# Small numbers in one shared tile, and the norms of queries and keys applied to the attention scores

## The chip, the cores and the metric

The kernel runs on one core of a Trainium2 chip. The metric is the time of one execution on the device in microseconds (us). The kernel before was timed in three runs: 2431.29, 2431.8 and 2432.54 us, median 2431.8 us.

## The reference

One layer of a streaming encoder on 256 tokens of width 2048, all in fp32. In order:

```
x += 1/2 * SwiGLU(norm(x))                  # d_ff = 5632, called ffn1 in the kernel
h  = norm(x); proj = h @ w_in               # six inputs of two recurrent branches, and gates
y_A = HGRN2 recurrence; y_B = conv(4) -> RG-LRU * gelu gate
x += (sigmoid(gate_A) * (y_A @ w_branch_a) + sigmoid(gate_B) * (y_B @ w_branch_b)) @ w_out
x += CrossAttention(norm(x), norm(mem))     # 4 heads of 512, 256 memory tokens
x += 1/2 * SwiGLU(norm(x))                  # called ffn2
return norm(x)
```

The part that the change rewrites is the cross-attention's scores:

```
q = norm(x) @ wq;  k, v = split(norm(mem) @ wkv)
s = einsum('bshd,bmhd->bhsm', q, k) * (512 ** -0.5)
p = softmax(s, axis=-1);  o = einsum('bhsm,bmhd->bshd', p, v);  x += o @ wo
```

A norm is `x * rsqrt(mean(x*x) + eps) * gain`. The gain works on a feature; the root works on a token, so it can be multiplied into any later result of a matrix product, row by row: for q, a row is a query token, for k a memory token.

## The kernel before

**Precision.** Every fp32 operand is split in two tiles, a rounded high part (`h`, `xh`, written by ACT) and the rest (`l`, `xl`, written by DVE as the difference), and a product of two numbers is three matmuls: high by high, high by low, low by high. A matmul here is 128 rows by 128 stationary columns by 512 (or 256) moving columns; its first operand in a row's name is what moves or what stays, the names are only sorted. Weights come in pieces of 1 MB (`raw`, 128x2048) over the queue of SP, are split by ACT and DVE, and are used by PE once. In the two feed-forward parts most pieces are multiplied by a scheme with seven instead of eight block products, for which DVE also makes differences (`td`, `made`) and splits them (`tl`).

**Order.** The program is first recorded as a list of operations. `Flow.arrange` then plays it through with a price for each operation and sets the order on every engine and the buffer that each tile takes; `Flow.emit` writes the instructions in that order. So one operation less or more can move others. All instructions carry line 478, where they are emitted; rows are told apart by the tiles' names.

**Places.** Tiles lie in pools, one behind the other in each partition, each tile starting on the next multiple of 32 bytes. In the built program before, the order is: constants (`vt`, `ones`, `eps`, the residual `x0` to `x3`, `rmtok`, `par`); nine tiles of 8192 bytes in the pool `big`; 24 tiles of 4096 bytes in `slots`; the small tiles (`sst`, `stdt`, `ssm`, `rtok`, `root`, `st`); then the scoped pools. In the feed-forward parts the scoped pool is `more`, four further tiles of 8192 bytes that are used as `big` ones are. In the middle it holds `tmp`, `scores`, `extra`, `feature`. Weights (`h`, `l`, `tl`) therefore lie in `big` or in `more`, as buffers come free; the other operand of a feed-forward matmul (`xh`, `xl`, `hidop`) lies in `slots`, and `ms`, the memory tokens, in `big` or `more`.

**The middle's norms.** `product` (the planner's queries, keys and input projection) gives 512 columns, 256 of high and 256 of low tokens; `summed` adds the two halves (ACT copies one to `lo`, DVE adds) and, with `by`, multiplies by a tile `rstd` of 128x256 that holds a token's root in each column. `by_feature` makes such a tile: two DVE operations write `diag`, an fp32 matmul with `ones` spreads it, ACT copies it out. `rtok` and `rmtok` hold the roots of the text and the memory tokens as columns, one number for each partition. `scores(h)` computes a head: for each of two groups of 128 queries, 4 x 2 matmuls, `summed` into `p`, the maximum of each row, its negative into `st`, ACT's exponential with that as bias, the reciprocal of the sum, and DVE's multiplication by it. Four transposes per head (`acc<-vt,p`) then turn `p` for the product with the values (`ps`, `vs`).

Of the kernel before, what the change touches and what calls it, by code (L numbers as in the profile page):

```python
# [9 lines left out]
F32 = mybir.dt.float32  # L10
F32R = mybir.dt.float32r
ACT = mybir.ActivationFunctionType
ALU = mybir.AluOpType

P = 128
T = 256
D = 2048
# [6 lines left out]
HD = D // HEADS  # L24
# [15 lines left out]
PAD = 16  # L40
# [149 lines left out]
class Flow:  # L190
# [22 lines left out]
    def pool(self, name, bufs, scope=None, **kw):  # L213
        self.pools.append(Pool(self, name, bufs, scope, **kw))
        return self.pools[-1]
# [267 lines left out]
def block_kernel(tc: tile.TileContext, xT, xin, memT, mem, vec, gfin, bgate, lruw, wu1, wd1, win, wv,  # L483
                 wg, wab, wout, wq, wk, wvm, wo, wu2, wd2, out_):
    flow = Flow(tc)
    pe, dve, act, sp, gps = flow.queues
    pool = flow.pool

    const = pool("const", 1)
    flow.share("big", pool("big", 9), 9)  # L490

    def big(name, dt=F32R):
        return flow.shared("big", [P, 2048], dt, name)

    slots = pool("slots", 24)
    small = pool("small", 2)
# [16 lines left out]
    def slot(dt=F32, name="slot"):  # L513
        return slots.tile([P, 1024], dt, name=name, tag="slot")

    def t1(name="t1"):
        return scoped["tmp"].tile([P, T], F32, name=name, tag="t1")

    def bank(name="acc"):
        return psum.tile([P, 512], F32, name=name, tag="acc")  # L520
# [6 lines left out]
    def col(name, i=0, n=1):  # L527
        a = VEC[name][0] + i
        return vt[:, a:a + n]
# [3 lines left out]
    warm = bank("warm")  # L533
    for _ in range(16):
        pe.matmul(warm[:, :P], ones, ones, start=True, stop=True)
    eps = const.tile([P, 1], F32, name="eps")
    act.activation(eps, ones[:, :1], ACT.Copy, scale=EPS)
    xt = [const.tile([P, 4 * T], F32, name=f"x{q}") for q in range(4)]
    x = [xt[k // 4][:, (k % 4) * T:(k % 4 + 1) * T] for k in range(KT)]
# [57 lines left out]
    def weights(*key):  # L597
        while plan and len(ahead) < 2:
            i = next(planned)
            k, src, kind = plan.pop(0)  # L600
            flow.room = room["scope"] if k[0] in orders else None
            if i in head:
                head[i]()
            if plan and plan[0][2] == "added":
                begun.append(begin_added(plan[0][1]))
            ahead.append((k, prepare(src, kind, 4 if i < 4 else 1)))
            if i in rest:
                rest[i]()
            make_ahead(i - between[0])
        k, w = ahead.pop(0)  # L610
        assert k == key, (k, key)
        return w
# [72 lines left out]
    def product(xs, w, late=()):  # L685

        acc = bank()
        h, l = w

        def high(ks):  # L690
            for k in ks:
                pe.matmul(acc, h[:, k * P:(k + 1) * P], xs[k], start=k == 0, stop=False)

        def low(ks):
            for k in ks:
                done["product"] = pe.matmul(acc[:, :T], l[:, k * P:(k + 1) * P], xs[k][:, :T], start=False,
                                            stop=k == KT - 1).ins

        high(range(KT - 4))
        was_late = bool(late)  # L700
        if was_late:
            flush(late)
            low(range(KT - 4))
        high(range(KT - 4, KT))
        low(range(KT - 4 if was_late else 0, KT))
        return acc
# [15 lines left out]
    def summed(acc, out=None, by=None):  # L722

        lo = t1("lo")
        act.activation(lo, acc[:, T:], ACT.Copy)
        out = t1("sum") if out is None else out
        dve.tensor_tensor(out=out, in0=acc[:, :T], in1=lo, op=ALU.add)
        if by is not None:
            dve.tensor_tensor(out=out, in0=out, in1=by, op=ALU.mult)
        return out  # L730
# [105 lines left out]
    def by_feature(r):  # L836

        diag = t1("diag")
        for t in range(2):
            dve.tensor_scalar(out=diag[:, t * P:(t + 1) * P], in0=ident, scalar1=r[:, t:t + 1], scalar2=None,  # L840
                              op0=ALU.mult)
        acc = bank()
        pe.matmul(acc[:, :T], ones, diag, start=True, stop=True)
        o = scoped["feature"].tile([P, T], F32, name="rstd", tag="rstd")
        act.activation(o, acc[:, :T], ACT.Copy)
        return o
# [233 lines left out]
            self.tiles.append(self.cur[:, i * 512:(i + 1) * 512])  # L1080
            return self.tiles[-1]

    ms1, rmtok = BigOperands(), const.tile([P, 2], F32, name="rmtok")

    def head_memory(kq):
        m = slot(name="mem")
# [4 lines left out]
                ms1.add(m[:, j:j + T], col("mem_norm", 4 * kq + j // T))  # L1091

    def head_squares():
        ss = small.tile([P, 2 + PAD], F32, name="ssm", tag="ssm", bufs=1)[:, :2]
        for t in range(2):
            m = big("memory", F32)
            sp.dma_start(m, mem[t])
            act.activation(m, m, ACT.Square, accum_out=ss[:, t:t + 1])
        act.activation(ss, ss, ACT.Sqrt, bias=eps, scale=1.0 / D)
        dve.reciprocal(out=rmtok, in_=ss)  # L1100

    head.update({kq: lambda kq=kq: head_memory(kq) for kq in range(4)})
    todo = [[] for _ in range(11)]
    for p in range(8):
        todo[p].append(lambda p=p: head_x(p))
        if p % 2:
            todo[p].append(lambda p=p: sums1[p // 2]())
    todo[3].append(head_squares)
    for c in range(4):
        todo[6 + c].append(lambda c=c: head_residual(c))  # L1110
# [75 lines left out]
    def pump(n):  # L1186
        while n > 0 and side:
            try:
                n -= n if next(side[0]) else 1
            except StopIteration:  # L1190
                side.pop(0)

    def heads(t):
        return t.rearrange("p (h t) -> p h t", h=4)
# [280 lines left out]
    xs3, sq3 = Operands(), TokenSquares()  # L1475
# [12 lines left out]
    qs = Operands()  # L1488
    ms = Operands()
    for m in range(KT):  # L1490
        acc = product(xs3.tiles, weights("q", m), late)
        if m == 0:
            rstd = by_feature(sq3.rstd_tokens())
            dve.tensor_scalar(out=rstd, in0=rstd, scalar1=HD ** -0.5, scalar2=None, op0=ALU.mult)
        qs.add(summed(acc, by=rstd))
        for i in range(2 * m, 2 * m + 2) if m < 4 else (m + 4,) if m < 12 else ():
            if i % 4 == 0:
                mt = slot(name="mem")
                sp.dma_start(mt, memT[:, i * T:(i + 4) * T])
            mk = heads(mt)[:, i % 4]  # L1500
            ms.add(mk, col("mem_norm", i))
    probs, ks, vs = {}, Operands(), {}

    def scores(h):
        p = slot(name="p")
        pv = p.rearrange("p (t m) -> p t m", t=4)
        for t in range(2):
            acc = bank()
            for j in range(4):
                d = h * 4 + j  # L1510
                a, b = t * P, T + t * P
                pe.matmul(acc, qs.tiles[d][:, a:a + P], ks.tiles[d], start=(j == 0), stop=False)
                pe.matmul(acc[:, :T], qs.tiles[d][:, b:b + P], ks.tiles[d][:, :T], start=False, stop=(j == 3))
            s = summed(acc, out=pv[:, t])
            st = small.tile([P, 4], F32, name="st", tag="st", bufs=4)
            dve.tensor_reduce(out=st[:, 0:1], in_=s, axis=mybir.AxisListType.X, op=ALU.max)
            dve.tensor_scalar(out=st[:, 1:2], in0=st[:, 0:1], scalar1=-1.0, scalar2=None, op0=ALU.mult)
            act.activation(s, s, ACT.Exp, bias=st[:, 1:2], accum_out=st[:, 2:3])
            dve.reciprocal(out=st[:, 3:4], in_=st[:, 2:3])
            dve.tensor_scalar(out=s, in0=s, scalar1=st[:, 3:4], scalar2=None, op0=ALU.mult)  # L1520
            yield
        acc = bank()
        for mt in range(2):
            for t in range(2):
                pe.transpose(acc[:, mt * T + t * P:][:, :P], pv[:, t, mt * P:(mt + 1) * P], ident)
        ps = slot(F32R, "ps")
        psv = ps.rearrange("p (m t) -> p m t", m=2)
        av = acc.rearrange("p (m t) -> p m t", m=2)
        act.activation(psv[:, :, :T], av, ACT.Copy)
        dve.tensor_tensor(out=psv[:, :, T:], in0=av, in1=psv[:, :, :T].bitcast(F32), op=ALU.subtract)  # L1530
        probs[h] = ps
        yield

    def take_values(g):
        f = slot(name="values")
        sp.dma_start(f, values[g])
        for t in range(2):
            s = slot(F32R, "vs")
            r = f[:, t * 512:(t + 1) * 512]
            split(s[:, :512], s[:, 512:], r)  # L1540
            vs[g, t] = s

    for m in range(KT):
        acc = product(ms.tiles, weights("k", m))
        if m == 0:
            rmem = by_feature(rmtok)
        ks.add(summed(acc, by=rmem))
        if m % 4 == 3:
            side.append(scores(m // 4))
            take_values(m // 4)  # L1550
        pump(1)
# [3 lines left out]
    for h in range(HEADS):  # L1555
        for j in range(4):
            acc = bank()
            for t in range(2):
                ps = probs[h][:, t * 512:(t + 1) * 512]
                s = vs[h, t]  # L1560
# [144 lines left out]
```

## Time and profile before

| | |
|---|---|
| median of three runs | 2431.8 us |
| profiled execution, its own time | 2431.7 us |
| its span, first to last instruction | 2429.9 us |
| TensorE clock granted, mean | 0.999 |
| PE busy | 2419.3 us, 12105 records |
| DVE busy | 2090.5 us |
| ACT busy | 1442.8 us |
| HBM traffic over the span | 265 GB/s |

The profile is of one execution; its time is 0.1 us from the median. "Busy" of PE overlaps, since a matmul of 393 ns starts about 227 ns after the one ahead of it: how fast PE goes is read from the starts, not from the durations. By stages the span is about: ffn1 0 to 775 us, the branches to 1200, gates and output product to 1450, queries and keys with scores to 1650, output of the attention to 1745, ffn2 to the end.

### The profile page before, as it was taken

Reading aid. Unit: us, or ns where it says so; the run is one execution under the profiler, and the core shown is the slowest. Engines: PE = TensorE matmul, PEld = TensorE weight load, DVE = VectorE, ACT = ScalarE, POOL = GpSimd, SP = SyncE. Lnnn points to the kernel's source line nnn. Section 1 sums busy time; section 2 is a strip of 40 time slices with the busy share of each in tenths; the row PEclk is TensorE's granted clock in tenths of the full one; section 3 lists DMA queues with packets and bytes.
Section 4 is the critical chain, followed back from the end, with each engine's and each line's share of the span. In section 5 each row is a group of like instructions: output and inputs, shape, how many; then the busy total and the mean of one; then the engine's idle time right before and its main releaser. Section 6 shows DMA issues by size and latency. Waiting matters only on the chain. (4 is left out here: it accounts for less than half of the span.)

```text
span 2429.9 us, 31006 instructions
## 1 busy us (share of the span) xinstructions
PE 2419.3 (100%) x12105; PEld 2005.8 (83%) x12105; DVE 2090.5 (86%) x2270; ACT 1442.8 (59%) x1432; POOL 88.6 (4%) x149
## 2 busy tenths in 40 slices
PE   9999999999999999999999999999999999999998
PEld 8888788888888888888888888888878788888887
DVE  7899999999996677888787878887789999999994
ACT  8765666666665544445853455555676666665563
POOL 0000000000000000000000000000000000000000
PEclk9999999999999999999999999999999999999999
DMA  9675877777774578798898898887798667667773
GB/s 364 242 274 180 260 259 255 249 258 248 254 256 177 182 290 325 268 349 330 328 339 329 327 372 337 331 312 260 291 372 299 255 247 264 257 258 259 260 273 113
DMA packets 101235, 674.37 MB, mean 278 GB/s; under 512 B 11232, under 2 KB 12000, under 8 KB 27232
## 3 DMA queue, kind: packets, MB, share of 16 engines
q1 hardware_dynamic: 79776, 523.40, 57.5%
q0 software_dynamic: 20592, 147.86, 18.9%
q8 instruction: 95, 1.56, 0.2%
q10 hardware_dynamic: 720, 1.13, 0.1%
q14 instruction: 52, 0.43, 0.0%
HBM read 581.12 MB, written 62.91 MB: 265 GB/s over the span
## 5 line engine op out<-in xcount | busy, mean ns | idle before, releaser
L478 DVE TENSOR_TENSOR l<-raw,h 128x2048 fp32r<-128x2048 f32 (+2 forms) x425 | 860.1, 2028 | 173.9 <-ACT h L478 80.3
L478 ACT ACTIVATE h<-raw 128x2048 fp32r<-128x2048 f32 (+2 forms) x425 | 722.1, 1705 | 383.5 <-PE acc L478 176.2
L478 PE MATMUL acc<-h,xh 128*128 128x512 f32 x1237 | 476.8, 393 | 0.5 <-DVE ev L478 0.3
L478 PE MATMUL acc<-h,xl 128*128 128x512 f32 x1237 | 475.5, 392 | 0.0
L478 ACT ACTIVATE h<-td 128x1024 fp32r<-128x1024 f32 (+1 forms) x262 | 322.9, 1241 | 227.9 <-DVE td L478 171.7
L478 DVE TENSOR_TENSOR tl<-td,h 128x1024 fp32r<-128x1024 f32 (+1 forms) x262 | 375.6, 1448 | 8.6 <-PE acc L478 5.2
L478 PE MATMUL acc<-h,hidop 128*128 128x512 f32 x1408 | 360.7, 394 | 0.0
L478 PE MATMUL acc<-h,ops 128*128 128x512 f32 x1408 | 336.9, 391 | 0.0
L478 PEld LDWEIGHTS acc<-h,hidop 128*128 128x128 f32 x1408 | 262.9, 188 | 58.8
L478 PEld LDWEIGHTS acc<-h,ops 128*128 128x128 f32 x1408 | 262.7, 188 | 54.0
L478 PE MATMUL acc<-ops,h 128*128 128x512 f32 x1152 | 282.1, 393 | 0.2 <-DVE ops L478 0.2
L478 PEld LDWEIGHTS acc<-h,xh 128*128 128x128 f32 x1237 | 232.0, 188 | 54.9 <-ACT h L478 1.6
L478 PEld LDWEIGHTS acc<-h,xl 128*128 128x128 f32 x1237 | 232.4, 188 | 51.6
L478 PEld LDWEIGHTS acc<-ops,h 128*128 128x128 f32 x1152 | 211.4, 188 | 42.4 <-DVE ops L478 0.6
L478 PE MATMUL acc<-l,hidop 128*128 128x512 f32 x704 | 195.7, 392 | 0.0
L478 PE MATMUL acc<-tl,xh 128*128 128x512 f32 x636 | 177.4, 395 | 0.6 <-DVE tl L478 0.6
L478 PE MATMUL acc<-l,ops 128*128 128x512 f32 x704 | 174.3, 389 | 0.0
L478 PE MATMUL acc<-l,xh 128*128 128x512 f32 x601 | 169.8, 393 | 0.0
L478 DVE TENSOR_TENSOR made<-made 128x512 f32<-128x512 f32 x224 | 152.2, 688 | 9.1 <-DMA made<-wu 5.7
L478 PEld LDWEIGHTS acc<-l,hidop 128*128 128x128 f32 x704 | 132.2, 188 | 29.8
L478 PEld LDWEIGHTS acc<-ops,l 128*128 128x128 f32 x1152 | 150.5, 191 | 6.4
L478 PEld LDWEIGHTS acc<-l,ops 128*128 128x128 f32 x704 | 132.1, 188 | 27.4
(172 smaller groups left out, 2135.3 us busy)
## 6 DMA issues: line engine op xcount, KB each, us to landing
raw<-wu SPq DMA_DIRECT2D x109, 1024.0 KB, 6.2
raw<-wd SPq DMA_DIRECT2D x72, 1024.0 KB, 6.6
made<-wu POOLq DMA_DIRECT2D x56, 1024.0 KB, 6.7
kept<-made POOLq DMA_DIRECT2D x56, 1024.0 KB, 6.9
td<-kept SPq DMA_DIRECT2D x56, 1024.0 KB, 7.2
raw<-wu SPq DMA_DIRECT2D x56, 768.0 KB, 5.8
raw<-win SPq DMA_DIRECT2D x40, 1024.0 KB, 4.9
raw<-wg SPq DMA_DIRECT2D x32, 1024.0 KB, 6.6
```

The source lines that it names most:

```text
L478: getattr(op.queue.real, method)(*map(real, args), **{k: real(v) for k, v in kw.items()})
```

## The change

`eps`, `rmtok`, the sums of squares of the memory tokens (`ssm`, until now a padded tile of the small pool) and a new pair of columns `scale` become slices of one constant tile `few` of 128x8. `rmtok` no longer has a place behind `x3`, and `ssm` none among the small tiles, so everything behind them moves:

| first byte of the first tile | before | after | past a multiple of 256, before | after |
|---|---|---|---|---|
| `big` | 20,128 | 20,096 | 160 | 128 |
| `slots` | 93,856 | 93,824 | 160 | 128 |
| scoped pools (`more`, `tmp`, ...) | 192,768 | 192,640 | 0 | 128 |

All tiles of 1 KB and more in a pool share its figure, and the slices that matmuls read start at multiples of 512 bytes in them.

Queries and keys are no longer multiplied when they are summed. The root of a memory token, `rmem`, is multiplied into the scores (`by=rmem`); the root of a query token, times 512 ** -0.5, is the column `scale`, and goes into the exponential as its scale and into the negative maximum. `by_feature` is called once less.

```diff
-    eps = const.tile([P, 1], F32, name="eps")
+    few = const.tile([P, 8], F32, name="few")
+    eps, rmtok, ssm, scale = few[:, :1], few[:, 1:3], few[:, 3:5], few[:, 5:7]
...
-    ms1, rmtok = BigOperands(), const.tile([P, 2], F32, name="rmtok")
+    ms1 = BigOperands()
...
-        ss = small.tile([P, 2 + PAD], F32, name="ssm", tag="ssm", bufs=1)[:, :2]
...
-            act.activation(m, m, ACT.Square, accum_out=ss[:, t:t + 1])
-        act.activation(ss, ss, ACT.Sqrt, bias=eps, scale=1.0 / D)
-        dve.reciprocal(out=rmtok, in_=ss)
+            act.activation(m, m, ACT.Square, accum_out=ssm[:, t:t + 1])
+        act.activation(ssm, ssm, ACT.Sqrt, bias=eps, scale=1.0 / D)
+        dve.reciprocal(out=rmtok, in_=ssm)
...
         if m == 0:
-            rstd = by_feature(sq3.rstd_tokens())
-            dve.tensor_scalar(out=rstd, in0=rstd, scalar1=HD ** -0.5, scalar2=None, op0=ALU.mult)
-        qs.add(summed(acc, by=rstd))
+            dve.tensor_scalar(out=scale, in0=sq3.rstd_tokens()[:, :2], scalar1=HD ** -0.5, scalar2=None, op0=ALU.mult)
+        qs.add(summed(acc))
...
-            s = summed(acc, out=pv[:, t])
+            s = summed(acc, out=pv[:, t], by=rmem)
...
-            dve.tensor_scalar(out=st[:, 1:2], in0=st[:, 0:1], scalar1=-1.0, scalar2=None, op0=ALU.mult)
-            act.activation(s, s, ACT.Exp, bias=st[:, 1:2], accum_out=st[:, 2:3])
+            dve.tensor_scalar(out=st[:, 1:2], in0=st[:, 0:1], scalar1=scale[:, t:t + 1], scalar2=-1.0,
+                              op0=ALU.mult, op1=ALU.mult)
+            act.activation(s, s, ACT.Exp, bias=st[:, 1:2], scale=scale[:, t:t + 1], accum_out=st[:, 2:3])
...
-        ks.add(summed(acc, by=rmem))
+        ks.add(summed(acc))
```

The order changes only between the last piece of the output product and the building of ffn2's operands; the matmuls of both feed-forward parts, and the splits of their weights, stand as they did. On PE, at the first product of the queries, there stood before (`diag` with `ones` is the spreading matmul, `x_304` the last transposes of the residual, `ops` with `h` and `l` the queries):

```order
L478 MATMUL acc<-vt,x_304 128x128 x8
L478 MATMUL acc<-ops,l 128x256 x12
L478 MATMUL acc<-ops,h 128x512 x6
L478 MATMUL acc<-ops,l 128x256 x4
L478 MATMUL acc<-ops,h 128x512 x2
L478 MATMUL acc<-diag,ones 128x256
L478 MATMUL acc<-ops,h 128x512 x12
```

and now:

```order
L478 MATMUL acc<-vt,x_304 128x128 x8
L478 MATMUL acc<-ops,l 128x256 x12
L478 MATMUL acc<-ops,h 128x512 x6
L478 MATMUL acc<-ops,l 128x256 x4
L478 MATMUL acc<-ops,h 128x512 x14
```

The spreading matmul in the second product is gone; the one for the memory tokens stands, as before, ahead of the keys. On DVE, for one group of 128 queries of the last head, there stood before:

```order
L478 TENSOR_TENSOR p<-acc,lo 128x256
L478 TENSOR_TENSOR ops<-sum,ops 128x256
L478 TENSOR_REDUCE st<-p 128x1
L478 TENSOR_TENSOR sum<-acc,lo 128x256
L478 TENSOR_SCALAR st<-st 128x1
```

and now:

```order
L478 TENSOR_TENSOR p<-acc,lo 128x256
L478 TENSOR_TENSOR p<-p,rstd 128x256
L478 TENSOR_TENSOR sum<-acc,lo 128x256
L478 TENSOR_REDUCE st<-p 128x1
L478 TENSOR_TENSOR sum<-acc,lo 128x256
L478 TENSOR_SCALAR st<-st,few 128x1
```

One multiplication by `rstd` has come into the chain ahead of the maximum. On PE, at the transposes of the last head's `p`, inside the output product (`h`, `ops`), there stood before:

```order
L478 MATMUL acc<-ps,vs 128x256
L478 MATMUL acc<-h,ops 128x512 x10
L478 MATMUL acc<-vt,p 128x128 x4
L478 MATMUL acc<-h,ops 128x512 x6
L478 MATMUL acc<-l,ops 128x512 x3
```

and now:

```order
L478 MATMUL acc<-ps,vs 128x256
L478 MATMUL acc<-h,ops 128x512 x14
L478 MATMUL acc<-vt,p 128x128 x4
L478 MATMUL acc<-h,ops 128x512 x2
L478 MATMUL acc<-l,ops 128x512 x7
```

The transposes stand four matmuls of the output product later.

## The prediction, made before the changed kernel was run

> **What bounds the kernel.** I read the page first, then PE's list of waits.
>
> ```profile
> span 2429.9 us, 31006 instructions
> PE 2419.3 (100%) x12105; PEld 2005.8 (83%) x12105; DVE 2090.5 (86%) x2270; ACT 1442.8 (59%) x1432; POOL 88.6 (4%) x149
> ...
> PE warm L478 <- DVE ones L478: 1.1, 1, 1.1
> PE acc L478 <- DVE tl L478: 0.6, 3, 0.2
> PE acc L478 <- ACT ms L478: 0.4, 1, 0.4
> ```
>
> PE is busy all the time, and the three longest of its waits make 2.1 us. So the end is set by how fast matmuls follow each other, and a step elsewhere counts only if it makes PE wait. The question is whether matmuls follow each other equally fast everywhere. The timeline answers: the first column is a group's start, so the spacing is the next start less this one, divided by the count. In the output product, where no tile of `more` exists:
>
> ```profile
> 1301.88 1.98 PE L478 MATMUL acc<-l,ops 128*128 128x512 f32 x8
> 1303.69 3.79 PE L478 MATMUL acc<-h,ops 128*128 128x512 f32 x16
> 1307.32 1.98 PE L478 MATMUL acc<-l,ops 128*128 128x512 f32 x8
> ```
>
> 24 matmuls in 5.44 us, 227 ns each. Early in ffn1, the products of memory tokens (`ms`) and value weights:
>
> ```profile
> 12.82 3.79 PE L478 MATMUL acc<-h,ms 128*128 128x512 f32 x16
> 16.45 1.98 PE L478 MATMUL acc<-l,ms 128*128 128x512 f32 x8
> 18.27 3.84 PE L478 MATMUL acc<-h,ms 128*128 128x512 f32 x16
> 21.94 2.03 PE L478 MATMUL acc<-l,ms 128*128 128x512 f32 x8
> 23.81 0.39 PE L478 MATMUL acc<-h,ms 128*128 128x512 f32 x1
> ```
>
> The layout of the built program says where each lies. The first two groups read both operands in `big`: 227 ns. The third reads both in `more`: 3.67 us for 16, 229 ns. The fourth reads weights in `big` and `ms` in `more`: 1.87 us for 8, 234 ns. The same in ffn2:
>
> ```profile
> 1804.16 0.87 PE L478 MATMUL acc<-l,xh 128*128 128x512 f32 x3
> 1804.87 1.10 PE L478 MATMUL acc<-tl,xh 128*128 128x512 f32 x4
> 1805.81 0.39 PE L478 MATMUL acc<-h,xh 128*128 128x512 f32 x1
> ...
> 1809.02 0.84 PE L478 MATMUL acc<-l,xh 128*128 128x512 f32 x3
> 1809.70 1.10 PE L478 MATMUL acc<-tl,xh 128*128 128x512 f32 x4
> 1810.64 0.39 PE L478 MATMUL acc<-h,xh 128*128 128x512 f32 x1
> ```
>
> The `l` at 1804.16 and both `tl` lie in `more`, `xh` in `slots`: 237, 235 and 235 ns. The `l` at 1809.02 lies in `big`: 0.68 us for three, 227 ns, with the same names and code. The 14 matmuls between 1805.81 and 1809.02 read weights in `big`, yet take 229 ns each: behind a mixed group the spacing is disturbed for about nine matmuls (some 30 ns in all, here 3.21 us less 14 x 226.7 ns = 36 ns), then steady. A pair is slow, then, when its two operands start at different distances past a multiple of 256 bytes (0 and 160), in either direction; it is not the address of one of them.
>
> **The change, part by part.**
>
> *The places.* After the change `big`, `slots` and `more` all start 128 past a multiple of 256. By the layouts, 1,978 of the 9,571 matmuls of 128x512 are mixed before and none after. The first mixed group is the one at 21.94, the last one is this:
>
> ```profile
> 2419.05 2.03 PE L478 MATMUL acc<-h,hidop 128*128 128x512 f32 x8
> 2420.92 1.08 PE L478 MATMUL acc<-l,hidop 128*128 128x512 f32 x4
> ```
>
> (1.87 us for 8, 234 ns). Over all records: 1,962 mixed ones are under 260 ns to the next start, and lie 7.26 ns on average over the steady 226.7, together 14.2 us. The 16 others are interrupted and I leave them. The 1,903 unmixed ones within nine places behind a mixed run (295 runs, the first at 23.81) lie 3.9 ns over, together 7.5 us. Both disappear if equal distances are what matters. Other interruptions (the transposes of `hidop`, a wait) leave the same tail, about 25 ns where no mixed group cuts it short; with 61 of them in the two feed-forward parts, 1.5 us of tails remain, of which 0.7 are counted elsewhere today. So 0.8 us come back: 14.2 + 7.5 - 0.8 = 20.9 us. Bounds: 14 (if the tails come from something else) and 21.7.
>
> One rule speaks against this. The Trainium skill, "TensorE: Matmul & The Clock Gate" (Part 2, step 1), has PE read its two operands through two independent ports, so that loading the next weights takes nothing from the running matmul. By that the two places could not matter to each other, and this term would be 0; the 227 and 237 ns of `l` with `xh` above disagree with it.
>
> *What stays within PE's cover.* Splits and differences on DVE and ACT show no dependence on place in the trace; they are beside PE, as are the DMAs.
>
> *The spreading matmul.*
>
> ```profile
> 1452.13 0.63 PE L478 MATMUL acc<-ops,h 128*128 128x512 f32 x2
> 1452.59 0.60 PE L478 MATMUL acc<-diag,ones 128*128 128x256 f32 x2
> 1452.84 3.08 PE L478 MATMUL acc<-ops,h 128*128 128x512 f32 x12
> ```
>
> Removed from PE's path: 0.25 us by the starts, 0.60 by its duration. I take 0.4, since the next group starts under its end and pays for the switch. With it go two DVE operations on `diag`, ACT's copy and DVE's scaling, all beside PE.
>
> *DVE's and ACT's part of the attention.*
>
> ```profile
> L478 DVE TENSOR_TENSOR sum<-sum,rstd 128x256 f32<-128x256 f32 x56 | 23.6, 423 | 1.2
> L478 DVE TENSOR_TENSOR p<-acc,lo 128x256 f32<-128x256 f32 x8 | 3.4, 419 | 0.4 <-ACT lo L478 0.4
> L478 ACT ACTIVATE p<-p,st 128x256 f32<-128x256 f32 x8 | 4.0, 505 | 3.4 <-DVE st L478 3.4
> L478 ACT ACTIVATE ops<-sum 128x256 fp32r<-128x256 f32 x48 | 19.8, 413 | 28.7 <-DVE sum L478 28.5
> L478 ACT ACTIVATE ops<-mem,vt 128x256 fp32r<-128x256 f32 x16 | 6.9, 503 | 0.0
> ```
>
> 32 multiplications of 423 ns leave the 56, 8 come to the scores: DVE does 10.2 us less. None of it is on PE's path. But the chain of a score grows by 0.42 us, and by up to 0.09 in the exponential (the copy of `ops` takes 413 ns without and 503 with a column as scale). Queued behind the new multiplication on DVE are sums that free PE's banks; PE waits for `p` at the transposes. The tightest is the last head:
>
> ```profile
> 1648.09 0.36 DVE L478 TENSOR_SCALAR p<-p,st 128x256 f32<-128x256 f32 x1
> ...
> 1648.94 0.60 PE L478 MATMUL acc<-vt,p 128*128 128x128 f32 x4
> ```
>
> 0.5 us of room. Two groups lengthen that head by up to 1.0 us, but its transposes now stand four matmuls later (0.9 us), and four multiplications of the last keys are gone from DVE ahead of it. I take 0.2 us; the bounds are 0 and 8 x 0.51 = 4.1. SP's moved loads (`mem`, `values`, one weight earlier or later) and POOL's sums stay in a stretch where the list of PE's waits is empty; at nothing, and if that cover went, a late weight costs the part of its transfer that PE then waits for.
>
> *What is late next.* A faster PE has less room over DVE. By stretches, DVE is the third figure:
>
> ```profile
> 100.00:700.00 600.00, 599.42 (x2642) 488.46 (x2641) 563.46 (x565) 395.58 (x323) 21.38 (x25) 1.00 0.76 247
> 240.00:300.00 60.00, 59.42 (x259) 47.07 (x258) 59.05 (x62) 41.37 (x33) 3.48 (x4) 1.00 0.82 252
> 1740.00:1770.00 30.00, 30.00 (x135) 24.29 (x134) 27.83 (x28) 27.34 (x27) 0.00 (x0) 1.00 1.01 409
> 1830.00:1860.00 30.00, 30.00 (x137) 24.51 (x136) 29.64 (x22) 22.14 (x15) 0.00 (x0) 1.00 0.95 348
> 1890.00:1920.00 30.00, 30.00 (x133) 23.29 (x131) 29.54 (x24) 18.90 (x16) 0.00 (x0) 1.00 0.84 318
> 1920.00:1950.00 30.00, 29.82 (x134) 24.16 (x133) 29.93 (x32) 17.53 (x16) 0.00 (x0) 1.00 0.52 193
> 1850.00:2400.00 550.00, 549.81 (x2421) 447.53 (x2420) 523.66 (x446) 332.40 (x259) 0.00 (x0) 1.00 0.69 255
> ```
>
> Most of the feed-forward parts leave DVE 5 to 6% idle, against a gain there of 1.4%. But at 240 to 300 and about 1830 to 1980 DVE is full, and at 1740 to 1770 the DMAs are. The chain of waits shows it:
>
> ```profile
> 1918.07 2.30 DVE tl L478
> ...
> 1920.42 501.60 PE acc L478 x2210
> ```
>
> Up to 1920 the end hangs on a DVE operation. The part of the 20.9 us that falls into 0 to 60, 240 to 300 and 1740 to 1980 is 0.4 + 0.8 + 3.9 = 5.1 us (excess of the records in those stretches). Between losing none and all of it I take 2.0: DVE still has some idle time there (0.46 us in 1890 to 1920), so part can be used.
>
> Sum, against the profiled execution's 2431.7 us, 0.1 from the median: 2431.7 - 20.9 - 0.4 + 0.2 + 2.0 = 2412.6.
>
> **The rivals.**
> 1. DVE takes over. If its in-order queue holds PE up in all of the feed-forward parts, say for half the gain: 2431.7 - 10.5 - 0.4 + 0.2 = 2421.0. For it: 94 to 95% busy. Against: the long stretches have three to four times as much idle as PE gains.
> 2. The places don't matter, so that the change does nothing to PE but drop a matmul; mixed pairs are slow for another reason that stays, such as `more` lying far from `slots`. Time: 2431.7 - 0.4 + 0.2 = 2431.5. Against: `ms` and weights both in `more` went at 229, mostly a tail. (The rule of the Trainium skill named above would have it end here.)
> 3. Slower: the new distance itself is worse. If 128 past 256 costs every one of the 9,571 matmuls the 229.4 ns of the group at 18.27 instead of 226.7, that is +25.8 us, and with tails and mixed ones gone (-21.7) the time is 2431.7 + 25.8 - 21.7 - 0.4 + 0.2 = 2435.6; it decides from 2.3 ns each. Against: that group's 40 ns over are one tail of about 36. No row has 128.
> 4. The longer score chain stalls PE at each head: + 4.1 us instead of 0.2, 2416.5. Against: the later transposes.
>
> **How the numbers follow.** The forecast has 0.66, with its own range of 2409 to 2417; rival 1 has 0.15, rival 4 0.07, rival 2 0.05, rival 3 0.07. A measurement of this kernel tells changes over 0.2% (4.9 us) from none. Forecast and rivals 1 and 4 are faster by more: 0.88. Rival 2 is the same: 0.05; rival 3 slower: 0.07. The predicted time is the forecast's, 2412.6. The range is 2408.5 to 2422: below, the whole 21.7 of places, the matmul at 0.6 and no loss (2409.4) and a little for waits that go; above, rival 1 with a microsecond more. It leaves rivals 2 and 3 out.
>
> **What would show it.** In the profile after, groups of `l` or `tl` with `xh` at 227 ns wherever they lie, and 229 only behind transposes; the stretch 1850 to 2400 some 8 us shorter; PE's list of waits with DVE `tl` at about 2 us, mostly around what is 1900 now; one `diag` product less. Spacings of 229 everywhere would mean rival 3, 234 in the old places rival 2, long waits for `tl` or `l` rival 1, waits for `p` or `ps` rival 4. The forecast is wrong if the slow pairs have another cause than unequal distances.

## The result, and the profile after

The changed kernel takes 2418.3 us (median of six runs, 2416.82 to 2419.16) against 2431.84 us of the kernel before: a ratio of 0.9943, 95% interval 0.9931 to 0.9956. The forecast was 2412.6 us with a range of 2408.5 to 2422: the direction and this range held, the gain is 13.5 us where 19.2 were forecast, and the narrower range of the forecast alone, 2409 to 2417, was missed by 1.3 us. The profiled execution took 2416.82 us. Its page, first the lines that answer to those of before, then PE's list of waits (us in total, times, longest):

```profile
span 2415.0 us, 30977 instructions
PE 2401.8 (99%) x12103; PEld 2003.9 (83%) x12103; DVE 2080.2 (86%) x2244; ACT 1441.9 (60%) x1431; POOL 88.3 (4%) x149
```

```profile
PE warm L478 <- DVE ones L478: 1.1, 1, 1.1
PE acc L478 <- DVE ops L478: 1.0, 2, 0.8
PE acc L478 <- DVE tl L478: 0.7, 3, 0.3
PE acc L478 <- DVE x L478: 0.7, 1, 0.7
PE acc L478 <- DVE l L478: 0.4, 1, 0.4
PE acc L478 <- DVE ev L478: 0.3, 1, 0.3
PE acc L478 <- ACT h L478: 0.2, 1, 0.2
```

PE is still busy nearly all the time, but the list of its waits has grown: `x` and `l` are new in it, and `ops` stood at 0.2 us, all three from DVE. The timeline of PE shows the spacing at the matmuls that were mixed. It is the same place in ffn2 that the prediction showed (first figure: start; second: length of the group; the spacing is the next start less this one, by the count):

```profile
1796.58 0.84 PE L478 MATMUL acc<-l,xh 128*128 128x512 f32 x3
1797.26 1.07 PE L478 MATMUL acc<-tl,xh 128*128 128x512 f32 x4
1798.17 0.39 PE L478 MATMUL acc<-h,xh 128*128 128x512 f32 x1
...
1801.34 0.84 PE L478 MATMUL acc<-l,xh 128*128 128x512 f32 x3
```

From start to start: 0.68 us for three and 0.91 us for four, 227 ns each, where 237 and 235 stood. The 14 matmuls from 1798.17 to 1801.34 take 3.17 us, 226.4 each: the tail of about 36 ns behind the mixed group is gone too. The chain of waits, with the start and the length of each step:

```profile
1909.81 2.30 DVE tl L478
...
1912.15 494.31 PE acc L478 x2210
```

The last 2,210 matmuls, the same ones, take 494.31 us instead of 501.60. Two stretches by their busy times, in which the first figure behind the length is PE's and the third DVE's:

```profile
100.00:700.00 600.00, 598.15 (x2666) 492.09 (x2665) 567.78 (x570) 399.89 (x326) 21.53 (x26) 1.00 0.76 248
240.00:300.00 60.00, 59.30 (x263) 47.20 (x263) 59.12 (x61) 41.96 (x36) 3.47 (x4) 1.00 0.87 261
```

In 100 to 700 us PE is busy 1.27 us less than before, in a stretch of the same length: it waits there now.

I took the starts of all 128x512 matmuls apart. An interval under 260 ns counts as *spacing*, with what it has over 226.7 ns; a longer one as an *interruption*, also with its excess. Between the first and the last matmul start, before against after:

| us | before | after | difference | the forecast's term |
|---|---|---|---|---|
| spacing, all parts | 25.8 | 5.2 | -20.6 | -20.9 |
| ffn1 and ffn2: interruptions | 8.0 | 11.5 | +3.5 | +2.0, with the next row |
| ffn1 and ffn2: other instructions (mostly transposes, and the 5 us at the start up to the first 128x512) | 25.4 | 26.1 | +0.8 | |
| middle, gates to the attention's output (whole length) | 613.6 | 614.4 | +0.8 | -0.2 (matmul -0.4, chain +0.2) |
| behind the last matmul | 8.3 | 9.0 | +0.7 | 0 |
| sum | | | -14.8 | -19.1 |

The sum is the difference of the two profiled executions (2431.7 - 2416.8 = 14.9). The matmuls gave what they were to give. What is missing was lost in three other places: in the feed-forward parts, in the middle and behind the last matmul. About 0.4 us of the feed-forward rows is the start of the kernel, where the first matmul of 128x512 begins at 6.57 us instead of 6.15. In the profiles of all the kernels below it begins between 6.1 and 7.6 us, at 6.57 and at 7.28 in two profiles of the changed kernel itself, so this part is put down to spread and not to the change.

### The profile page after: what moved, and what is told of

It is laid out like the page before. It is cut to its first block, busy times and chain, and to the rows that moved or that the text cites. A ratio compares the mean times of both kernels' runs of the same rounds, so it can differ in the third digit from the quotient of the medians.

```text
span 2415.0 us, 30977 instructions
## 1 busy us (share of the span) xinstructions
PE 2401.8 (99%) x12103; PEld 2003.9 (83%) x12103; DVE 2080.2 (86%) x2244; ACT 1441.9 (60%) x1431; POOL 88.3 (4%) x149
## 3 DMA queue, kind: packets, MB, share of 16 engines
q0 software_dynamic: 20592, 147.86, 19.1%
## 5 line engine op out<-in xcount | busy, mean ns | idle before, releaser
L478 PE MATMUL acc<-h,hidop 128*128 128x512 f32 x1408 | 355.7, 390 | 0.0
```

The costliest lines, as they stand in the source:

```text
L478: getattr(op.queue.real, method)(*map(real, args), **{k: real(v) for k, v in kw.items()})
```

## The experiments

In the table, "interruptions" are those of ffn1 and ffn2, "middle" is the length of the part from the gates to the attention's output, and spacing and interruptions are worked out from one profile as above. Times are medians with their range. The profile of the queries' half is of its fastest run (2412.8 us).

| kernel | us | spacing | interruptions | middle |
|---|---|---|---|---|
| before | 2431.8 (2431.3-2432.5) | 25.8 | 8.0 | 613.6 |
| changed | 2418.3 (2416.8-2419.2) | 5.2 | 11.5 | 614.4 |
| places only | 2415.0 (2413.3-2415.4) | 5.0 | 10.5 | 613.5 |
| attention only | 2434.3 (2432.8-2435.8) | 25.9 | 7.0 | 615.5 |
| `big` 32 bytes off | 2456.0 (2455.95-2456.05) | 53.0 | 6.0 | 625.8 |
| scoped pools 128 off | 2429.0 (2428.0-2431.8) | 20.0 | 7.5 | 614.3 |
| places only, less DVE | 2408.7 (2408.5-2409.0) | 4.4 | 6.2 | 613.6 |
| before, less DVE | 2429.8 (2429.4-2430.2) | 25.8 | 5.7 | 614.6 |
| changed, queries' half | 2414.9 (2412.8-2415.2) | 4.9 | 9.8 | 612.7 |
| changed, keys' half | 2416.4 (2415.5-2417.1) | 5.2 | 12.2 | 614.3 |
| changed, again | 2416.9 (2416.6-2419.1) | 5.5 | 10.1 | 615.0 |
| queries' half, four more by DMA | 2413.7 (2413.3-2413.9) | 5.0 | 8.4 | 613.1 |
| queries' half, four more made ahead | 2439.4 (2437.9-2440.8) | 4.8 | 9.1 | 633.1 |
| changed, short score chain | 2416.1 (2415.7-2420.9) | 5.3 | 10.2 | 613.9 |

### The places alone

Against the kernel before, one number:

```diff
-        ss = small.tile([P, 2 + PAD], F32, name="ssm", tag="ssm", bufs=1)[:, :2]
+        ss = small.tile([P, 2 + PAD + 40], F32, name="ssm", tag="ssm", bufs=1)[:, :2]
```

> The kernel before with its attention code and its order of instructions untouched; only the unused tail of one small tile grows by 160 bytes, so that big, slots and the scoped pools all start 160 past a multiple of 256 (modulo 512 the scoped pools differ from the others by 256). Theory (a matmul is slowed when its two operands lie at different distances past a multiple of 256 bytes): no matmul is mixed, the 20.6 us of spacing over 226.7 ns that went in the change go here too, and the same 3 to 5 us of new waits come back, since DVE's work is the same: 2418 us, between 2416 and 2420. Rival, the change works by its new order in the attention and by the spreading matmul that is gone: no gain here, 2431.5. Rival, the distance counts modulo 512 or the region does: about 2431 too, with tl and l in the scoped pool still at 234 ns against xh.

Measured: 2414.96 us, ratio 0.9929 (0.9915 to 0.9942), below the expected 2416 to 2420. Every instruction stands where it stood before; 160 unused bytes give more than the whole change. The same place in ffn2:

```profile
1799.52 0.84 PE L478 MATMUL acc<-l,xh 128*128 128x512 f32 x3
1800.20 1.07 PE L478 MATMUL acc<-tl,xh 128*128 128x512 f32 x4
1801.11 0.39 PE L478 MATMUL acc<-h,xh 128*128 128x512 f32 x1
```

0.68 us for three, 0.91 for four: 227 ns, with `tl` in the scoped pool. So `more` isn't slow as a region; it lies where it lay, 160 bytes on. Equality modulo 256 is enough, since modulo 512 the two places still differ by 256. And it isn't the number 128 that counts: here all lie at 160. Rivals 2 and 3 of the prediction fall. The two independent read ports that the Trainium skill gives PE ("TensorE: Matmul & The Clock Gate", Part 2, step 1) don't make the two places independent of each other here: moving one of them changed 235 ns to 227.

### The attention's edit alone

Against the kernel before: the change's lines in the queries, keys and scores, and

```diff
-    eps = const.tile([P, 1], F32, name="eps")
+    few = const.tile([P, 8], F32, name="few")
+    eps, scale = few[:, :1], few[:, 5:7]
```

> The change's code in the queries, keys and scores alone (scale lies in the unused bytes behind eps), with every large tile at its address of before: 160, 160 and 0. The order of instructions is that of the changed kernel. Theory: the spacing stays as before, the spreading matmul gives 0.4 and the longer score chain costs 0.2 to 1.5 (the changed kernel shows two longer waits about its scores, at 1604 and 1632): 2431 to 2433 us, 2432 as the one number. Rival, the attention's part of the change carries the gain: 2418 to 2425.

Measured: 2434.29 us, ratio 1.0010 (1.0002 to 1.0019): a loss of 2.4 us, above the expected 2431 to 2433 us. PE's list of waits from 1440 to 1710 us, which was empty before:

```profile
PE acc L478 <- DVE ops L478: 0.8, 1, 0.8
PE acc L478 <- DVE p L478: 0.7, 2, 0.5
```

The middle is 1.9 us longer than before. This half of the change costs time, and places alone (2415.0) beat the whole (2418.3 and 2416.9).

### Other distances

Against the changed kernel, twice. First the tile of small numbers goes to a pool of its own between `big` and `slots`, so that `big` moves from 128 to 96:

```diff
-    slots = pool("slots", 24)
+    between_pool = pool("between", 1)
+    slots = pool("slots", 24)
...
-    few = const.tile([P, 8], F32, name="few")
+    few = between_pool.tile([P, 8], F32, name="few")
```

> The changed kernel with its tile of small numbers moved from ahead of the constants to between big and slots: big starts 96 past a multiple of 256, slots and the scoped pools 128 as before. 7,384 of the 9,571 matmuls of 128x512 now have operands at distances that differ by 32 bytes. Theory: each of them costs 7.26 ns more as the mixed ones did, 53.6 us, and tails and the 1,152 matmuls of 128x256 add up to 8: 2472 to 2480 us, with the groups of ops and h in the output product at 234 ns. Rival, a difference of 32 bytes doesn't count, only larger ones: 2418. Rival, only tiles of the scoped pool in combination with slots are slow: 2418.

Measured: 2456.0 us, ratio 1.0098 (1.0080 to 1.0117). The output product, steady before and after the change, is slow now:

```profile
1310.34 3.90 PE L478 MATMUL acc<-h,ops 128*128 128x512 f32 x16
1314.08 2.03 PE L478 MATMUL acc<-l,ops 128*128 128x512 f32 x8
1315.94 3.90 PE L478 MATMUL acc<-h,ops 128*128 128x512 f32 x16
```

3.74 us for 16 and 1.86 for 8: 234 and 232 ns, with weights in `big`, not `more`. The direction is as expected, the size is not: 16 to 24 us less. Three parts of that are measured: 32 bytes cost 6.5 ns over the steady spacing (233.2 on average over 7,296 records) and not 7.26; the interruptions of the feed-forward parts fell from 11.5 to 6.0 us; and the matmuls of 128x256 became faster (last section). Together they make some 14 us; the rest of the difference stays open.

Second, `st` grows so that the scoped pools lie 128 bytes off:

```diff
-            st = small.tile([P, 4], F32, name="st", tag="st", bufs=4)
+            st = small.tile([P, 16], F32, name="st", tag="st", bufs=4)
```

> The changed kernel with 128 unused bytes more among the small tiles: the scoped pools start at a multiple of 256, big and slots stay at 128 past one. The same pairs are mixed as in the kernel before, but by 128 bytes instead of 96. Theory with a period of 256: the 20.6 us come back and with them PE has its old slack over DVE, so most of the 3.7 us of new interruptions go: 2418.3 + 20.6 - 3.7 = 2435, between 2431 and 2439. Rival, the period is 128 or less: 2418.

Measured: 2429.0 us, below the expected 2431 to 2439; ratio 0.9990 (0.9980 to 1.0000). In ffn2:

```profile
1802.67 0.86 PE L478 MATMUL acc<-l,xh 128*128 128x512 f32 x3
1803.37 1.09 PE L478 MATMUL acc<-tl,xh 128*128 128x512 f32 x4
1804.30 0.39 PE L478 MATMUL acc<-h,xh 128*128 128x512 f32 x1
```

0.70 us for three, 0.93 for four: 233 and 232 ns. So the period isn't 128 nor a part of it; with the steady spacing at 256, in the run of the places alone, it is 256. By 128 bytes a mixed matmul costs 5.6 ns on average (232.3, 1,961 records), by 96 bytes 7.3. Spacing (+14.8) and interruptions (-4.0) together make 10.8 us more than in the changed kernel. The profiled executions differ by 11.5 us (2428.3 - 2416.8), the medians by 10.7.

### Less work for DVE

Against the kernel with the places alone, and in the same way against the kernel before; `cut` takes the first columns of all operands when the instruction is written, so the order stays, and what those sums would add in the other columns is left out of the result:

```diff
-                        dve.tensor_tensor(out=o, in0=accs[n], in1=x, op=ALU.add)
+                        dve.tensor_tensor(out=o, in0=accs[n], in1=x, op=ALU.add, cut=128)
...
-                                                                    op0=ALU.mult, op1=ALU.add).ins
+                                                                    op0=ALU.mult, op1=ALU.add, cut=128).ins
```

> The kernel with the places alone changed (2415.0 us), with the order of all engines kept, but three of the additions that empty each group's banks in the feed-forward parts and all additions to the residual there work on 128 instead of 512 columns: DVE has some 34 us less to do in each feed-forward part (81 operations by 0.42 us), and part of the sums is left out of the result. Theory (the interruptions that came with the faster spacing are DVE's queue being late): the 10.5 us of interruptions in the two feed-forward parts fall towards the 6.0 that they had in the run with the slowest spacing: 2410 to 2412 us. Rival, they are weights or ACT being late, or the transposes themselves: 2414.5 to 2415.5.

> The same relief of DVE in the kernel before, at 160, 160 and 0. Theory: PE is slower there and DVE less often late (8.0 us of interruptions in the feed-forward parts), so that there is less to win: 2430 to 2431 us, against 3 to 5 us with equal places. Rival, the relief works as much at any spacing: 2427 to 2428.

Measured: 2408.67 us (ratio 0.9903, 0.9890 to 0.9917) with equal places, 6.3 us less than without the relief, and 2429.77 (0.9991, 0.9982 to 1.0000) at the old ones, 2.0 us less. The first is below the expected 2410 to 2412, the second just below 2430 to 2431. The stretch 100 to 700 us, first with the places alone and then with the relief:

```profile
100.00:700.00 600.00, 599.00 (x2672) 493.14 (x2671) 569.25 (x571) 401.06 (x328) 22.19 (x26) 1.00 0.76 248
```

```profile
100.00:700.00 600.00, 599.63 (x2684) 496.51 (x2683) 548.96 (x574) 401.61 (x328) 22.19 (x26) 1.00 0.77 249
```

DVE falls from 95 to 91%, and 12 matmuls more fit in. Of the 6.3 us, 4.3 are interruptions of the feed-forward parts, 0.6 the spacing (the tails behind them), and 0.4 lie behind the last matmul, where the shorter addition stands too, as it does in the relieved kernel with old places. What remains of interruptions is about 6 us at either spacing, as much as in the slowest kernel above. So the theory holds: those over 6 us are DVE late, 2 us of them before the change and 4.5 to 5.5 with equal places. The additions that were shortened are partly those on which PE waits, so this pair of runs does not tell the load of DVE's queue from the length of these operations.

The timeline of the changed kernel shows one of them in ffn1, PE first, then DVE:

```profile
430.44 0.39 PE L478 MATMUL acc<-h,xl 128*128 128x512 f32 x1
431.50 0.50 PE L478 MATMUL acc<-h,xh 128*128 128x512 f32 x1 [0.68 <-DVE x L478]
```

```profile
428.50 0.68 DVE L478 TENSOR_TENSOR td<-raw,td 128x512 f32<-128x512 f32 x1
429.10 1.75 DVE L478 TENSOR_TENSOR l<-raw,h 128x1536 fp32r<-128x1536 f32 x1
430.76 0.68 DVE L478 SCALAR_TENSOR_TENSOR x<-acc,x 128x512 f32<-128x512 f32 x1
```

The addition to `x`, which empties a bank that PE wants next, stands behind `l` on DVE and starts when `l` is done. It is 1.06 us between two starts where 0.23 is usual. Before the change no interval around 368, 402, 418, 430 and 460 us is over 290 ns; after it ten are, together 2.3 us over 226.7 each. With less for DVE none of them is left.

### The two halves of the attention's edit

Against the changed kernel; the first diff undoes the keys' half and leaves the queries', the second the other way round:

```diff
-            s = summed(acc, out=pv[:, t], by=rmem)
+            s = summed(acc, out=pv[:, t])
...
-        ks.add(summed(acc))
+        ks.add(summed(acc, by=rmem))
```

```diff
-            dve.tensor_scalar(out=scale, in0=sq3.rstd_tokens()[:, :2], scalar1=HD ** -0.5, scalar2=None, op0=ALU.mult)
-        qs.add(summed(acc))
+            rstd = by_feature(sq3.rstd_tokens())
+            dve.tensor_scalar(out=rstd, in0=rstd, scalar1=HD ** -0.5, scalar2=None, op0=ALU.mult)
+        qs.add(summed(acc, by=rstd))
...
-            act.activation(s, s, ACT.Exp, bias=st[:, 1:2], scale=scale[:, t:t + 1], accum_out=st[:, 2:3])
+            act.activation(s, s, ACT.Exp, bias=st[:, 1:2], accum_out=st[:, 2:3])
```

(with the negative maximum as before in the second).

> The changed kernel with the keys' half of the attention edit undone: the keys are multiplied by rmem when they are summed, as before, and the scores are not; the queries' root stays in the exponential, the spreading matmul stays away. Theory (the stalls of the attention come from the new order around the last keys and from the multiplication in the scores): without that multiplication the score chain is as short as before, so this stands at the kernel with the places alone, less the matmul: 2414.5 to 2416 us. Rival, the queries' half costs the time: 2418.

> The changed kernel with the queries' half undone: queries are multiplied by the spread root as before (two spreading matmuls again), the memory tokens' root is multiplied into the scores. Theory: the stalls at the scores stay, and the matmul comes back: 2418 to 2419.5 us. Rival, the queries' half costs the time: 2415.

Measured: 2414.94 us (0.9928, 0.9914 to 0.9941) with the queries' half, as expected, 2416.38 (0.9934, 0.9922 to 0.9947) with the keys' half, which is below the 2418 to 2419.5 that were expected. The queries' half costs nothing: its middle is the shortest of all, 0.8 us under places only. With the keys' half the middle is 1.6 us longer than with the queries' half. The medians of the whole change lie 2.0 and 3.4 us above the queries' half. So the loss comes with the keys' half, that is with the multiplication in the scores and the order that comes with it. Each half has an order of its own, and the two don't add up exactly. It was also expected that the waits at the scores stay with the keys' half, and they don't: PE's list from 1440 to 1700 us is empty for either half alone. So the waits for `ops` and `p` come only with the order of the whole change, and where the keys' half alone loses its time in the middle no run here says.

### The change once more

> The changed kernel, untouched, beside the two that follow. The feed-forward parts of the kernels with equal places have the same instructions in the same order, but single waits there differ by up to 1.3 us between profiles (835 and 1,063 ns around 420 to 430 us in the changed kernel, none and 625 with the places alone). If these waits come and go between executions, this profile has another pattern of them and the runs spread over 2 us or more, with a median of 2417.5 to 2419. If they belong to the program, the pattern is the same as in its first profile and the runs agree within 1 us.

Measured: 2416.9 us (2416.61 to 2419.07), ratio 0.9941 (0.9927 to 0.9954). Four of five runs agree within 0.6 us, the fifth is 2 us longer. Both theories get a part. The wait at 430 us was 1,063 ns and is 1,124 in this profile; the interval of 835 ns at 418 us isn't there, and one of 719 ns at the transposes of `p` is new. So some waits belong to the program and others come and go. Over both sets the 11 runs of this kernel lie between 2416.6 and 2419.2, so that about a microsecond of the distance between the forecast and 2418.3 is spread; both profiled executions took 2416.8 or 2416.9.

### The score chain, shortened

Against the changed kernel, with `cut` as above:

```diff
-            s = summed(acc, out=pv[:, t], by=rmem)
+            s = summed(acc, out=pv[:, t], by=rmem, cut=16)
```

> The changed kernel in its own order, but the new multiplication of the scores by the memory tokens' root works on 16 of the 256 columns (the rest of that scaling is left out): each of the eight score chains is shorter by about 0.33 us. In the profiles of the changed kernel PE waits 0.5 us for p at the transposes (in one of two) and 0.8 us at 1632 for the last keys, which stand on DVE behind a split of weights of 2.28 us. Theory: the multiplication makes the wait for p, the order makes the wait for the keys: the first goes, the second stays at 0.8, and the time is about 2416.5, between 2416 and 2417. Rival, the multiplication makes both: no wait of either kind, 2415 to 2415.5. Rival, neither: 2416.9 as the changed kernel.

Measured: 2416.11 us (0.9941, 0.9927 to 0.9954), in the expected 2416 to 2417, though not to be told from 2416.9 by the times. The lists of waits tell it. From 1440 to 1700 us, first the second profile of the changed kernel, then the short chain (its lines are numbered four higher):

```profile
PE acc L478 <- DVE ops L478: 0.8, 1, 0.8
PE acc L478 <- DVE p L478: 0.5, 1, 0.5
```

```profile
PE acc L482 <- DVE ops L482: 0.8, 1, 0.8
```

The wait for `p` is gone, the wait for the last keys stays to the tenth. The first profile of the changed kernel had no wait for `p` either, so one profile is weak evidence for that half; the second half is firm. Where the wait for the keys comes from is seen on DVE in the changed kernel, with PE's row behind:

```profile
1630.11 2.28 DVE L478 TENSOR_TENSOR l<-raw,h 128x2048 fp32r<-128x2048 f32 x1
...
1632.31 0.75 DVE L478 TENSOR_TENSOR ops<-sum,ops 128x256 fp32r<-128x256 f32 x2
...
1632.78 1.66 PE L478 MATMUL acc<-ops 128*128 128x512 f32 x8 [0.83 <-DVE ops L478]
```

The last keys' low part stands behind a split of the next product's weights, which no one needs yet. That is the new order, not a price of the new multiplication.

### Relieving DVE by other means

Both against the kernel with the queries' half. Four more pieces of ffn1's down weights by an accumulating DMA:

```diff
-            if name == "ffn1" and e[0] == "down" and 0 < e[1] < NG - 2 and (e[3] + e[4] - e[1]) % 2 == 0:
+            if name == "ffn1" and e[0] == "down" and 0 < e[1] < NG - 2 and (e[3] == 1 or (e[3] + e[4] - e[1]) % 2 == 0):
```

> The kernel with the queries' half of the attention edit (2414.9 us), and four more pieces of down weights in ffn1 (20 instead of 16) whose low part is made by an accumulating DMA and a copy on ACT instead of by DVE: 4 x 2.28 us less for DVE there, 4 x 1 MB more of accumulating transfers. Theory (DVE late in ffn1): a quarter of the relief that gave 3.0 us in ffn1, so 0.8 us: 2413.5 to 2415. Rival, the transfers make weights late: 2416 or more. With 0.8 us the result may not be told from none.

Measured: 2413.68 us (0.9925, 0.9913 to 0.9938), within the expected 2413.5 to 2415 and the fastest kernel here beside the one with less for DVE, 3.2 us under the repeat of the changed kernel on the same chip. It beats both kernels of this case. Its five runs lie within 0.6 us. Against the queries' half it is 1.3 us in the medians, with ranges that overlap; in the profiles the interruptions of ffn1 fall from 5.0 to 3.6 us, but the other instructions there take 1.8 us more, of which 1.2 are a later start (the first matmul of 128x512 at 7.54 us, not 6.32), so the gain over that kernel isn't shown.

Four more pieces with differences made ahead:

```diff
-MADE = [(g, p) for g in range(NG) for p in range(8) if p in ((0, 2, 4, 7) if g > 2 else range(8))]
+MADE = [(g, p) for g in range(NG) for p in range(8) if p in ((0, 2, 4, 7) if g > 3 else range(8))]
```

> The kernel with the queries' half of the attention edit (2414.9 us), and all eight instead of four pieces of ffn2's group 3 with their differences made ahead, in the middle. DVE does 4 x 2.3 us less about 1900 to 1960 us and 4 x 2.7 us more in the middle, where it has room; 4 x 0.75 MB more are loaded in ffn2 and 4 x 1.75 MB moved in the middle. Theory: PE's waits around 1906 to 1955 fall by about a microsecond: 2413.5 to 2415. Rival, the middle's makers or the loads make PE wait there: 2416 or more.

Measured: 2439.4 us (1.0030, 1.0019 to 1.0042), the rival. ffn2 did get 2.3 us shorter, with interruptions of 2.8 instead of 4.7 us. But the middle lost 20 us and more. DVE, then PE:

```profile
1229.32 1.40 DVE L478 SCALAR_TENSOR_TENSOR gate<-acc,rtok,bgate 128x512 f32<-128x512 f32 x2
1244.17 2.87 DVE L478 TENSOR_TENSOR made<-made 128x512 f32<-128x512 f32 x4 [13.45 <-DMA made<-wu]
1246.96 4.49 DVE L478 TENSOR_TENSOR l<-raw,h 128x2048 fp32r<-128x2048 f32 x2
```

```profile
1249.30 2.08 PE L478 MATMUL acc<-l,ops 128*128 128x512 f32 x4 [10.09 <-DVE l L478]
```

The differences stand ahead of `l` on DVE and wait 13.45 us for their own load, and PE waits 10.09 us for an `l` that only queues behind them. DVE was not short of time there, it was blocked in order. From 1100 to 1450 us PE waits 14.7 us for `l` in three waits and 2.1 us for `h`, and behind them its matmuls go slower for a while (last section).

## Why the prediction was right, and where it was off

- *The places, -20.9:* right, in mechanism and size (-20.6). The mixed ones, their tails and the rest of the tails behind other interruptions came out as summed. The places alone gave the whole gain, in an order of instructions that didn't change.
- *Rivals 2 and 3 (the places don't matter; 128 itself is worse):* both fell. Equal places at 128 and at 160 give the same spacing, 5.2 and 5.0 us over the steady one.
- *What is late next, +2.0:* right in kind, wrong in place, and too small: 4.3 us in the first profile, of which 0.4 are the later start. In the repeat's profile it is about 2.5 without the start, so the size is known to about a microsecond. The step that failed is the sentence that most of the feed-forward parts leave DVE 5 to 6% idle against a gain of 1.4%, so that only the full stretches were charged. PE's wait for `tl`, which was to be about 2 us, stayed at 0.7. Instead 2.3 us (1.7 in the repeat) were lost around 368 to 460 us, where DVE's mean leaves enough room, because an operation on which PE waits can stand behind a split of 1.75 us. In this kernel the queue was late at single places while its mean was not full. Rival 1 (half of the gain eaten everywhere) went too far: of 20.6 us an eighth to a fifth was lost that way.
- *The spreading matmul and the score chain, -0.4 + 0.2:* the sign was wrong. The middle became 0.8 us longer in one profile and 1.4 in the other, 1.9 with the old places. The step looked only at the tightest head's chain and took the new order to be a help (the transposes four matmuls later). The chain did cost PE some tenths for `p` in some of the profiles. The larger wait, 0.8 to 0.9 us in every profile with the whole change's order, is for the last keys, which the new order puts behind a split of weights; the forecast had no term for that. Rival 4 named the place but not this mechanism. The queries' half, to which the spreading matmul belongs, does gain: in two profiles (with and without the four more by DMA) its middle is 0.4 and 0.8 us shorter than with the places alone.
- *Behind the last matmul, 0:* 0.7 us longer, and 0.4 to 0.7 us in every kernel with a part of the attention's edit and all of DVE's work, but not with the places alone. No run here says why.
- *What stays:* of the 5.7 us between 2412.6 and 2418.3, the terms above make 0.3 + 2.3 + 1.0 + 0.7 = 4.3 against the profiled execution; the rest is the distance of that execution from its median, and the second set of runs had its median at 2416.9.

## What to carry to other kernels

When PE sets the end, read its matmul starts by tile and by address before anything else: here the place of four buffers, set by 160 unused bytes, was worth 17 us, and the arithmetic that came with it a loss of 2 to 3. When a bound engine gets faster, don't compare its gain with another engine's mean idle time; look for the operations on which it waits and for what stands ahead of them in that engine's queue. A part of a change that "takes work away" is measured by itself, since a planner answers it with a new order.

## What the runs showed of the hardware that was not expected

- The price of unequal places depends on the distance. Mean spacing of 128x512 fp32r matmuls modulo 256: 227.2 ns at distance 0 (tails included), 233.2 at 32, 234.0 at 96, 232.3 at 128. Which of the two operands is ahead makes no difference at 32 or 96 (the same 233.2 and 234.0 either way, to 0.1 ns). A distance of 64 was not tried.
- For 128x256 matmuls it is the other way round. The queries' products, first in the changed kernel (equal places), then with `big` 32 bytes off:

```profile
1460.82 3.82 PE L478 MATMUL acc<-ops,h 128*128 128x512 f32 x16
1464.48 2.08 PE L478 MATMUL acc<-ops,l 128*128 128x256 f32 x16
1466.39 3.82 PE L478 MATMUL acc<-ops,h 128*128 128x512 f32 x16
```

```profile
1484.44 3.89 PE L478 MATMUL acc<-ops,h 128*128 128x512 f32 x16
1488.18 2.03 PE L478 MATMUL acc<-ops,l 128*128 128x256 f32 x16
1490.04 3.89 PE L478 MATMUL acc<-ops,h 128*128 128x512 f32 x16
```

The 16 of 256 columns take 1.91 us with equal places and 1.86 with unequal ones, 119.4 and 116.3 ns each; over the 1,057 of them that follow one another the means are 119.5 and 116.8. That is 3 us in the other direction. A kernel in which only these have unequal places was not tried.
- In the kernel with four more pieces made ahead, PE's granted clock fell during its waits. The stretch around them, with the granted clock behind the five busy times:

```profile
1200.00:1260.00 60.00, 43.23 (x161) 33.88 (x160) 40.88 (x46) 24.79 (x27) 5.90 (x11) 0.83 0.93 360
```

0.83 over 60 us, against 1.00 in the same stretch of the kernel that it was made from. In steps of 2 us the trace shows three falls, to 0.50 at 1222 to 1224 us, 0.51 at 1236 to 1238 and 0.50 from 1242 to 1254. Matmuls start 427 ns apart there instead of 227. The first fall follows a wait of 2.60 us, the second waits of 1.98 and 2.10 us, and the third lies in and behind the wait of 10.09 us. The Trainium skill ("TensorE: Matmul & The Clock Gate", Part 1) has the clock fall to half once PE has been idle for a window of about 3.4 us. The third fall agrees; the first two came after shorter waits, and there the measurement decides. So a wait can cost more than its length, here from about 2 us on.
